# Seven block products in place of eight, in more slices of two feed-forward layers

## The chip, the cores and the metric

The kernel runs on one NeuronCore of a Trainium2 chip. The metric is the device time of one execution in microseconds (us). Engines: PE (TensorE, matmuls), PEld (its weight loads), DVE (VectorE), ACT (ScalarE), POOL (GpSimd), SP (SyncE, which here issues most DMAs).

## The reference

One inference step of a two-layer decoder, for a prompt of 1024 tokens and 8 single sample tokens that share all weights; the model width is 1024, everything is float32.

```
for l in 0, 1:
    hn  = rmsnorm(h, g[l][0])
    mix = (l == 0: gated linear recurrence   | l == 1: stick-breaking attention over a shared K/V)
          in parallel with attention over 256 memory tokens, then @ w_o[l]
    h   = h + rmsnorm(mix, g[l][1])
    h   = h + rmsnorm(swiglu(rmsnorm(h, g[l][2]), w_gu[l], w_down[l]), g[l][3])
    after layer 0: shared K/V = rmsnorm(h, g_kv) @ w_kv

swiglu(h, w_gu, w_down):
    gate, up = split(h @ w_gu)          # 1024 -> 2 x 2816
    return (silu(gate) * up) @ w_down   # 2816 -> 1024
```

Outputs are the residual streams, the recurrent states, the shared K/V and the memory K/V.

## The kernel before, in words

Activations lie transposed: 128 rows of the model dimension on the partitions, tokens along the free dimension. The tokens are cut in two halves, `g = 0` with 512 prompt tokens and `g = 1` with the other 512 and the 8 samples (520). `NG = [512, 520]`. All matmuls of projections are done in float32r with both operands split in a high and a low part (`split_w` and `split_to`: ACT makes the high part, DVE subtracts it), three matmuls for each product: high x high, high x low, low x high.

Code is written as generators, one `yield` after each step; `weave` mixes several of them in proportion to given weights, and so sets the order in which the instructions are traced. A scheduler of the language then orders the instructions of each engine by this order and by what is ready, on its own estimate of times. Queues are first in, first out.

The feed-forward of a half has 22 slices of 128 hidden units, grouped in five parts: `PARTS = [(0, 5), (5, 5), (10, 4), (14, 4), (18, 4)]` (first slice, count). Each part computes its slices (gate and up for each) and then multiplies by its rows of `w_down` for all eight blocks of 128 outputs, adding into `R`. There are three forms of a slice:

- Plain (`ffn.part` with `proj`, L218): 2 x 8 x 3 = 48 matmuls of 512 columns in the first half, or 96 of 260 in the second, in two PSUM tiles of two banks each (`mmp`). SiLU is made of Exp and Ln.
- Plain in four single banks (`gate_up_q`, L453): 96 matmuls of half the columns, SiLU from ACT's own table. Beside it `sums_w` makes the sums of activations that the third form needs, some steps after each matmul group (`side`, `steps`).
- Block (`gate_up_w`, L499): gate and up together are a 2 x 2 block matrix (512 rows of the model dimension each) times a 2 x 2 block matrix of activations (two halves of the model dimension, two halves of the tokens). Strassen's scheme in Winograd's form takes 7 block products instead of 8: 7 x 4 x 3 = 84 matmuls of half the columns. Four of the seven weights are sums of blocks of `w_gu`. They are made ahead in DRAM by `weight_sums`, eight DMAs for a part on POOL's queue, some of them accumulating; each first waits, by a one-column copy on POOL, for the tile in `now[0]`, so that the DMAs are spread over the work. The tiles `y`, `z`, `u` hold the sums of activations; `raws` and `spl` choose the buffers of the raw and the split weights.

`ffn_w` runs a feed-forward from part `first` on: `len(steps)` slices by `gate_up_q`, the rest by `gate_up_w`, and w_down in four single banks (L631; the last one of all, with other widths, L663). `set_banks(True)` closes the two-bank tiles and opens four single banks, `set_banks(False)` the other way; the new pool waits until the old one is free.

Before the change the block form is used only in the second half (`g = 1`): in layer 0 for slices 13 to 21, in layer 1 for slices 3 to 21. The other slices are plain. Around them, in order of time (second-half mixers `a1`, `b1`; first-half mixers `a0`, `b0`; `o0`, `o1` are out-projections with norms and residual):

1. `a0`: recurrence, memory attention, projection.
2. `a1.core()` beside part 0 of the first half's feed-forward in layer 0, then part 1 beside `a1.sample()` and `a1.gate()`.
3. `a1.merge()`, `a1.mem()` and `a1.mem_sample()` beside parts 2 and 3; then part 4 alone.
4. Shared K/V of the first half, `b0.heads()`; then `b0.sb()` and `b0.mem()` beside parts 0 and 1 of the second half's feed-forward in layer 0; then its parts 2 to 4 in `ffn_w`.
5. Shared K/V of the second half, `b1.heads()`; then `b1`'s attention and its samples beside parts 0 to 3 of the first half's feed-forward in layer 1.
6. `o1.mm()`, then `o1.finish()` beside part 4; then the last feed-forward in `ffn_w`, its parts 0 and 1 beside `f0.finish()` and the writing of rows.

In the samples' attention (`sample_scores`, `sample_pv`, L912 and L924) one 512 KB tile of the cache is loaded for each sample into the pool `c` (4 buffers), and DVE multiplies and reduces it. The evacuation of a w_down block into `R` is L390 (plain) or L640 (four banks).

## Time and profile before

| | |
|---|---|
| median of 3 runs | 2496.46 us (2495.56 to 2497.24) |
| the profiled execution | 2497.11 us |
| its span, first to last instruction | 2495.4 us |
| granted clock of TensorE over the span | 0.998 |
| PE, PEld busy | 2461.4, 2155.8 us |
| DVE, ACT, POOL busy | 1598.1, 1196.8, 121.9 us |
| matmuls | 15455 |
| HBM read, written | 358.76, 101.11 MB |

A matmul's record lasts from its start to a modelled end, so that records of neighbours overlap; "busy" is the time covered by at least one. The time from one matmul to the next is shorter than the mean of one and is read from long unbroken runs.

### The profile page before, as it was taken

How to read it: one execution, taken by the hardware profiler on the slowest of the kernel's cores; microseconds unless marked ns; L12 is line 12 of the kernel's file. 1: busy time of each engine (PE TensorE's matmuls, PEld its weight loads, DVE VectorE, ACT ScalarE, POOL GpSimd, SP SyncE). 2: the span in 40 equal slices, each digit the busy share in tenths (PEclk: the TensorE clock that was granted, in tenths of full speed). 3: DMA queues.
4: the chain of work that ended last, by engine and by line, in shares of the span. 5: the costliest groups of instructions: out<-in, count | busy, mean ns of one | idle time of the engine just before them, and what ended most of it. 6: DMA issues, size and time to landing. Idle time of an engine off the chain costs nothing.

```text
span 2495.4 us, 40868 instructions
## 1 busy us (share of the span) xinstructions
PE 2461.4 (99%) x15455; PEld 2155.8 (86%) x15455; DVE 1598.1 (64%) x2868; ACT 1196.8 (48%) x2289; POOL 121.9 (5%) x188
## 2 busy tenths in 40 slices
PE   8999999999999999999999999999999999999998
PEld 6888888877866898899999989977777798999998
DVE  5867556754765475665656575778677548855666
ACT  5437544243433454555544554555454345554445
POOL 1000000000010000000100100011000000000000
PEclk9999999999999999999999999999999999999999
DMA  5354666555786776566577746544343433464552
GB/s 190 111 165 119 162 184 157 132 141 150 223 204 184 197 185 194 165 156 167 134 199 193 226 140 187 160 145 144 102 140 119 122 120 114 141 186 144 148 148 73
DMA packets 521551, 391.26 MB, mean 157 GB/s; under 512 B 19973, under 2 KB 459858, under 8 KB 521354
## 3 DMA queue, kind: packets, MB, share of 16 engines
q1 hardware_dynamic: 493194, 308.94, 41.8%
q0 software_dynamic: 28160, 79.70, 13.5%
q8 instruction: 122, 2.00, 0.3%
q14 instruction: 75, 0.61, 0.1%
HBM read 358.76 MB, written 101.11 MB: 184 GB/s over the span
## 4 chain that ended last, share of the span: by engine, by line
PE 92%; DVE 4%; DMA 2%; ACT 1%; issue 1%; SPq 0%; DVEq 0%; ACTq 0%
PE mm L218 54%; PE q L499 11%; PE q L631 7%; PE s L1150 2%; PE mm L1018 2%; PE q L453 2%; PE s L1345 1%; PE s L1311 1%; PE s L885 1%; PE s L854 1%; PE mm L803 1%; PE mm L830 1%; PE q L663 1%; DMA c<-in_cache_mem_v 1%; PE ns L926 1%
## 5 line engine op out<-in xcount | busy, mean ns | idle before, releaser
L218 PE MATMUL mm<-x,ws 128*128 128x512 f32 (+1 forms) x6624 | 1215.0, 340 | 3.9 <-DVE r L390 1.5
L218 PEld LDWEIGHTS mm<-x,ws 128*128 128x128 f32 x6624 | 1012.5, 188 | 157.6 <-issue 14.6
L204 ACT CAST ws<-w 128x512 fp32r<-128x512 f32 (+1 forms) x672 | 395.3, 589 | 624.2 <-PE mm L218 477.8
L205 DVE TENSOR_TENSOR ws<-w,ws 128x512 fp32r<-128x512 f32 (+1 forms) x672 | 434.5, 650 | 270.5 <-ACT ws L204 263.8
L218 PE MATMUL mm<-m,ws 128*128 128x512 f32 (+1 forms) x1536 | 327.9, 366 | 4.7 <-DVE r L390 4.7
L218 PEld LDWEIGHTS mm<-m,ws 128*128 128x128 f32 x1536 | 253.2, 188 | 56.7 <-DVE r L390 7.3
L631 PE MATMUL q<-m,ws 128*128 128x260 f32 x1440 | 175.9, 283 | 0.0
L631 PEld LDWEIGHTS q<-m,ws 128*128 128x128 f32 x1440 | 173.4, 188 | 1.1 <-DVE t L522 0.5
L490 DVE TENSOR_TENSOR ws<-w,ws 128x512 fp32r<-128x512 f32 x164 | 112.4, 691 | 79.8 <-ACT ws L489 76.4
L489 ACT CAST ws<-w 128x512 fp32r<-128x512 f32 x164 | 101.4, 621 | 98.0 <-PE q L631 34.2
L499 PE MATMUL q<-x,ws 128*128 128x260 f32 x1008 | 134.3, 282 | 0.0
L499 PEld LDWEIGHTS q<-x,ws 128*128 128x128 f32 x1008 | 126.4, 188 | 0.0
L499 PE MATMUL q<-y,ws 128*128 128x260 f32 x912 | 119.3, 283 | 0.1
L499 PEld LDWEIGHTS q<-y,ws 128*128 128x128 f32 x912 | 113.5, 188 | 0.3 <-ACT q L506 0.3
L235 DVE TENSOR_SCALAR t<-mm 128x512 f32<-128x512 f32 (+1 forms) x70 | 48.3, 690 | 59.7 <-PE mm L218 59.4
L695 DVE TENSOR_TENSOR t<-t,mm 128x512 f32<-128x512 f32 (+1 forms) x54 | 37.2, 688 | 57.1 <-PE mm L218 57.1
L390 DVE TENSOR_TENSOR r<-r,mm 128x512 f32<-128x512 f32 (+1 forms) x72 | 49.3, 685 | 37.1 <-PE mm L218 36.2
L239 DVE TENSOR_TENSOR t<-t,t 128x512 f32<-128x512 f32 (+1 forms) x54 | 37.4, 692 | 55.1 <-ACT t L238 55.1
L226 DVE TENSOR_TENSOR m<-t,m 128x512 fp32r<-128x512 f32 (+1 forms) x88 | 60.9, 692 | 6.7 <-ACT m L225 5.3
L258 DVE TENSOR_TENSOR st<-st,n 128x512 f32<-128x512 f32 (+1 forms) x91 | 62.2, 691 | 3.0 <-ACT n L257 1.6
L225 ACT CAST m<-t 128x512 fp32r<-128x512 f32 (+1 forms) x88 | 54.9, 624 | 17.0 <-DVE t L695 7.7
L453 PE MATMUL q<-x,ws 128*128 128x260 f32 x480 | 61.0, 288 | 1.5 <-DVE ws L205 1.4
(344 smaller groups left out, 2850.5 us busy)
## 6 DMA issues: line engine op xcount, KB each, us to landing
w<-in_w_gu SPq DMA_DIRECT2D x310, 256.0 KB
w<-in_w_down SPq DMA_DIRECT2D x160, 256.0 KB
wsum<-in_w_gu POOLq DMA_DIRECT2D x36, 1024.0 KB, 9.4
w<-wsum SPq DMA_DIRECT2D x94, 256.0 KB
w<-in_w_in_a SPq DMA_DIRECT2D x80, 256.0 KB
w<-in_w_o SPq DMA_DIRECT2D x64, 256.0 KB
wsum<-in_w_gu POOLq DMA_DIRECT2D x12, 1280.0 KB, 11.4
wsum<-wsum POOLq DMA_DIRECT2D x12, 1024.0 KB, 5.6
```

What stands on the lines that cost most here:

```text
L204: nc.scalar.copy(ws[:, 0, :n, :], raw[:, :n, :])
L205: nc.vector.tensor_sub(ws[:, 1, :n, :], raw[:, :n, :], ws[:, 0, :n, :].bitcast(F32))
L218: nc.tensor.matmul(ps[:, a, : PW[g]], wt, xt[k][:, xi, o : o + PW[g]], start=(k == 0 and wi == 0), stop=(k == nk - 1 and wi == 2),)
L225: nc.scalar.copy(dst[0], src)
L226: nc.vector.tensor_sub(dst[1], src, dst[0].bitcast(F32))
L258: nc.vector.tensor_add(acc[:, :n], acc[:, :n], t[:, :n])
L453: ins = nc.tensor.matmul(pp[a][:, :h], wt, xt[k][:, xi, a * h : (a + 1) * h], start=(k == 0 and wi == 0), stop=(k == ND - 1 and wi == 2),)
L489: nc.scalar.copy(w[:, 0, :], src)
L490: nc.vector.tensor_sub(w[:, 1, :], src, w[:, 0, :].bitcast(F32))
L499: nc.tensor.matmul(ps[:, :h], w[:, wj, k * P : (k + 1) * P], x[:, xi, :], start=(first and k == 0 and wi == 0), stop=(k == 3 and wi == 2), ...
L631: nc.tensor.matmul(pp[a][:, :h], wt, mids[k][:, xi, a * h : (a + 1) * h], start=(k == 0 and wi == 0), stop=(k == nf - 1 and wi == 2),)
L1018: nc.tensor.matmul(pb[i][:, a, :], xt[k][:, xi, c * P : (c + 1) * P], ws[:, s, :], start=(k == 0 and wi == 0), stop=(k == ND - 1 and wi == 2),
```

## The change

It uses the block form for five slices of the first half in either layer (17 to 21), and for fourteen instead of nine of the second half in layer 0 (8 to 21). For that:

- `sums_w`, `gate_up_q`, `gate_up_w` and `ffn_w` take the half `g` as an argument; in the first half the columns are 256 + 256.
- Layer 0, first half: parts 3 and 4 run in an `ffn_w` of their own behind the memory attention of `a1`, with four single banks; part 2 alone stays beside that attention.
- Layer 0, second half: `ffn_w` begins with part 1 instead of part 2; part 0 alone stays beside `b0`'s attention.
- Layer 1, first half: parts 3 and 4 run in an `ffn_w` beside `o1.finish()`; parts 0 to 2 stay beside `b1`'s attention. There (`own`) the tiles `y` come from the pool `c`, and the split weights only from their own pool.
- `weight_sums` makes part 1 of layer 0 too (four parts, order 3, 4, 2, 1), and begins beside `a0.core()`, where `now[0]` is set to a tile of the recurrence. In layer 1 the order becomes 3, 4, 0, 1, 2, fewer steps stand in layer 0, and the last eight stand beside the last feed-forward's parts 0 and 1.

```diff
-    def sums_w(xs, ops, YT):
-        n, h = NG[1], PW[1]
+    def sums_w(g, xs, ops, YT, ZT):
+        n = NG[g]
+        h = n // 2
         for k in range(4):
             x0, x1 = xs[k], xs[k + 4]
             y = YT()
             if k % 2 == 0:
-                z, u = YT(), YT()
+                z, u = ZT(), ZT()
...
-    def gate_up_q(l, f, xt, side, n_side, first):
+    def gate_up_q(g, l, f, xt, side, n_side, first):
...
-    def gate_up_w(l, f, ops, spl, raws):
+    def gate_up_w(g, l, f, ops, spl, raws):
...
-        def __init__(self, l, x, steps, first, rows, R=None):
+        def __init__(self, g, l, x, steps, first, rows, R=None, own=False):
...
             def YT():
                 if rows:
                     return xpool.tile([P, 2, NG[1]], F32R, tag="x0", name=nm("y"))
+                if own:
+                    return cpool.tile([P, 2, 512], F32R, tag="c", name=nm("y"))
                 return A(F32R)
-            self.sums = sums_w(x, self.ops, YT)
+            self.sums = sums_w(g, x, self.ops, YT, YT if rows else lambda: A(F32R))
...
-            if (self.pi or not self.rows) and self.n % 8 in (1, 4, 6):
+            if (self.pi or not self.rows) and not self.own and self.n % 8 in (1, 4, 6):
                 return cpool.tile([P, 2, 512], F32R, tag="c", name=nm("ws"))
...
+                now[0] = F_[:, 0, 0:1]
                 for hh in range(2):
                     nc.vector.copy_predicated(
...
     drain(a0.v(), a0.fq())
+    w0 = weight_sums(0, (3, 4, 2, 1))
     weave(
-        (a0.core(), 22),
+        (a0.core(), 22), (islice(w0, 8), 8),
         (chain(mem_load(), mem_keys(0), mem_values(0), mem_keys(1), mem_values(1), a0.qm(M)), 22),
     )
...
-    w0 = weight_sums(0, range(2, 5))
...
-    ws = weight_sums(1, range(5))
-    weave(
-        (chain(a1.merge(), a1.mem()), 12), (a1.mem_sample(), 20), (chain(f0.part(2), f0.part(3)), 16),
-        (islice(ws, 11), 11),
-    )
-    weave((f0.part(4), 8), (islice(ws, 5), 5))
+    ws = weight_sums(1, (3, 4, 0, 1, 2))
+    weave((chain(a1.merge(), a1.mem()), 12), (a1.mem_sample(), 20), (f0.part(2), 8), (islice(ws, 4), 4))
+    set_banks(True)
+    fw = ffn_w(0, 0, o0.x, (5, 6, 5), 3, False, f0.R)
+    weave((chain(fw.part(3), fw.part(4)), 16), (islice(ws, 4), 4))
+    f0.acc = fw.acc
+    set_banks(False)
...
-    weave((chain(b0.sb(), b0.mem()), 25), (chain(f1.part(0), f1.part(1)), 18), (islice(ws, 16), 17))
+    weave((chain(b0.sb(), b0.mem()), 20), (f1.part(0), 9), (islice(ws, 16), 17))
     set_banks(True)
-    fw = ffn_w(0, o1.x, (5, 6, 5), 2, False, f1.R)
-    weave((chain(fw.part(2), fw.part(3), fw.part(4)), 24), (islice(ws, 8), 8))
+    fw = ffn_w(1, 0, o1.x, (5, 6, 5), 1, False, f1.R)
+    weave((chain(fw.part(1), fw.part(2), fw.part(3), fw.part(4)), 33), (islice(ws, 8), 8))
...
         (chain(b1.sb(), b1.mem()), 45), (chain(b1.sb_sample(), b1.mem_sample()), 39),
-        (chain(f0.part(0), f0.part(1), f0.part(2), f0.part(3)), 34),
+        (chain(f0.part(0), f0.part(1), f0.part(2)), 27),
     )
     o1 = out_proj(1, 1, A, True)
     drain(o1.mm(b1.xo))
-    weave((o1.finish(), 17), (f0.part(4), 8))
     set_banks(True)
-    f1 = ffn_w(1, o1.x, (5, 6, 5), 0, True)
-    weave((chain(f0.finish(False), store_y(0, f0.R), token_rows(1, o1.R)), 17), (chain(f1.part(0), f1.part(1)), 7))
+    fw = ffn_w(0, 1, o0.x, (5, 6, 5), 3, False, f0.R, True)
+    weave((o1.finish(), 17), (chain(fw.part(3), fw.part(4)), 16))
+    f0.acc = fw.acc
+    f1 = ffn_w(1, 1, o1.x, (5, 6, 5), 0, True)
+    weave((chain(f0.finish(False), store_y(0, f0.R), token_rows(1, o1.R)), 17), (chain(f1.part(0), f1.part(1)), 7), (ws, 4))
     drain(f1.part(2), f1.part(3), f1.part(4))
```

More of the change, by code (lines that the diff above doesn't have):

```diff
@@ L312, in rms_rows @@
         nc.vector.tensor_scalar(xt, xt, ss[:n], None, op0=ALU.mult)
-    made = [None]
+    made, now = [None], [None]
     def start(g, out):
@@ L440, in token_rows @@
         htok.append((ht, hs_))
-    def gate_up_q(l, f, xt, side, n_side, first):
-        h, n = PW[1], NG[1]
+    def gate_up_q(g, l, f, xt, side, n_side, first):
+        n = NG[g]
+        h = n // 2
         sg = T()
@@ L469, in gate_up_q @@
         return mt
-    def gate_up_w(l, f, ops, spl, raws):
-        h, n = PW[1], NG[1]
+    def gate_up_w(g, l, f, ops, spl, raws):
+        n = NG[g]
+        h = n // 2
         part, o = part_of(f)
@@ L527, in gate_up_w @@
         return mt
-    now = [None]
     act = [None]
@@ L563, in tile_decoder @@
     class ffn_w:
-        def __init__(self, l, x, steps, first, rows, R=None):
-            self.g, self.l, self.x, self.ops, self.steps, self.rows = 1, l, x, [], steps, rows
+        def __init__(self, g, l, x, steps, first, rows, R=None, own=False):
+            self.g, self.l, self.x, self.ops, self.steps, self.rows, self.own = g, l, x, [], steps, rows, own
             self.first, self.plain, self.n, self.r, self.pi = first, PARTS[first][0] + len(steps), 0, 0, 0
@@ L602, in part @@
         def part(self, pi):
-            l, n, h = self.l, NG[1], PW[1]
+            g, l, n = self.g, self.l, NG[self.g]
+            h = n // 2
             f0, nf = PARTS[pi]
@@ L609, in part @@
                 if f0 + j < self.plain:
-                    mids.append(gate_up_q(l, f0 + j, self.x, self.sums, self.steps[j], PARTS[self.first][0]))
+                    mids.append(
+                        gate_up_q(g, l, f0 + j, self.x, self.sums, self.steps[j], PARTS[self.first][0])
+                    )
                     now[0] = mids[-1][:, 0, 0:1].bitcast(F32)
                 else:
-                    mids.append(gate_up_w(l, f0 + j, self.ops, self.spl, self.raws))
+                    mids.append(gate_up_w(g, l, f0 + j, self.ops, self.spl, self.raws))
                 yield
```

## The prediction

> **What bounds the kernel now.** I read the page first: busy shares, then the engines of the chain that ended last.
>
> ```profile
> span 2495.4 us, 40868 instructions
> PE 2461.4 (99%) x15455; PEld 2155.8 (86%) x15455; DVE 1598.1 (64%) x2868; ACT 1196.8 (48%) x2289; POOL 121.9 (5%) x188
> PE 92%; DVE 4%; DMA 2%; ACT 1%; issue 1%; SPq 0%; DVEq 0%; ACTq 0%
> ```
>
> PE is idle for 2495.4 - 2461.4 = 34.0 us in all, and 92% of the chain is PE. So the time is the sum of the matmuls' spacings plus a few waits, and the change is to be priced by counting matmuls. "Busy" hides the spacing, since matmuls overlap in the records; a long unbroken run in the chain, its length divided by its count, gives it. In the chain in order of time (start, length, what, count):
>
> ```profile
> 652.85 55.64 PE mm L218 x240
> 1259.47 28.70 PE q L453 x240
> 1321.74 40.37 PE q L499 x336
> 1362.11 23.21 PE q L631 x192
> 1511.47 5.74 PE mm L218 x48
> ```
>
> The first run is the first half of the prompt, 512 columns: 55.64/240 = 231.8 ns. The others have 260 columns: gate/up of a plain slice in four banks 28.70/240 = 119.6, block products 40.37/336 = 120.1, w_down in four banks 23.21/192 = 120.9, the two-bank plain projection 5.74/48 = 119.6 ns. Two matmuls of 260 thus cost a little more than one of 512, while the block form does 7/8 of the work.
>
> What surrounds these runs, by windows (length, PE busy, PEld, DVE, ACT, POOL, clock, DMA share, GB/s):
>
> ```profile
> 690.00:828.00 138.00, 130.65 (x557) 96.46 (x556) 81.06 (x138) 50.22 (x106) 11.12 (x16) 1.00 0.73 190
> 1062.00:1250.00 188.00, 187.34 (x1446) 178.05 (x1445) 115.17 (x230) 98.03 (x203) 18.85 (x30) 1.00 0.62 153
> 1600.00:2000.00 400.00, 397.91 (x1824) 302.40 (x1822) 287.88 (x445) 193.11 (x372) 26.56 (x24) 1.00 0.43 127
> 2200.00:2430.00 230.00, 230.00 (x1917) 229.57 (x1916) 137.28 (x258) 114.39 (x233) 0.00 (x0) 1.00 0.56 161
> ```
>
> The first three are the stages from which the change takes feed-forward work that stands beside attention: call them A (memory attention of the second half and the samples, layer 0), B (stick-breaking of the first half, layer 1) and S (attention of the second half and the samples, layer 1). PE idles 7.35, 0.66 and 2.09 us in them. The last window holds block slices alone: no idle time at all, at 161 GB/s.
>
> **The change, part by part.** *First half, layers 0 and 1: slices 14 to 21 leave the plain form.* Their matmuls get 256 columns, a width that has no long run of its own. The nearest rows are the two widths of the last w_down, by form:
>
> ```profile
> L663 PE MATMUL q<-m,ws 128*128 128x264 f32 x96 | 12.1, 286 | 0.0
> L663 PE MATMUL q<-m,ws 128*128 128x256 f32 x96 | 11.9, 283 | 0.1
> ```
>
> Eight columns less are worth 0.2 us/96 = 2.1 ns of busy time or 3 ns of one's mean; four less, 1 to 1.5 ns. The slope between 512 and 260, (231.8 - 120.1)/252 = 0.44 ns a column, gives 1.8. I take 1.5: 118.1 plain, 118.6 block, 119.4 w_down. The far end is no saving from the narrower width. Per layer:
> - Slices 17 to 21, five: 48 x 231.8 = 11.13 us becomes 84 x 118.6 = 9.96, -1.17 each, -5.8.
> - Slices 14 to 16, three, plain in four banks so that the operand sums can be made beside them: 96 x 118.1 = 11.34, +0.21 each, +0.6.
> - w_down of parts 3 and 4: 96 x 231.8 = 22.25 becomes 192 x 119.4 = 22.92, +0.67 each, +1.3.
>
> That is -3.9 a layer, -7.7 for both; with no saving from the width (2 x 1092 x 1.5 ns) it is -4.4.
>
> *Second half, layer 0.* Block slices 8 to 21 instead of 13 to 21: five go from 96 matmuls at 119.6 (11.48) to 84 at 120.1 (10.09), -1.39 each, -7.0. Part 1's w_down keeps its count.
>
> Matmuls together: -14.7.
>
> *Operand sums*: `sums_w` now runs four times instead of two. One run, by groups of 1225 to 1265 us, and that window:
>
> ```profile
> L296 DVE TENSOR_TENSOR b<-b,b 128x260 f32<-128x260 f32 x16 | 6.7, 420 | 0.0
> L226 DVE TENSOR_TENSOR a<-b,a 128x260 fp32r<-128x260 f32 x16 | 6.6, 421 | 0.5 <-ACT a L225 0.5
> L288 DVE TENSOR_TENSOR b<-x 128x260 f32<-128x260 f32 x16 | 6.3, 420 | 0.0
> 1225.00:1265.00 40.00, 40.00 (x331) 39.57 (x330) 33.14 (x81) 19.44 (x44) 5.19 (x5) 1.00 0.95 226
> ```
>
> 19.6 us of DVE each, and PE lost nothing under it; without that cover it would be 19.6 each. One of the new runs stands alone (layer 0): 0. The other stands beside `o1.finish()`, whose DVE work competes; its nearest likeness is the same step in the last feed-forward:
>
> ```profile
> 2130.00:2187.00 57.00, 56.19 (x454) 55.61 (x455) 43.13 (x90) 29.71 (x68) 0.00 (x0) 0.97 0.51 151
> ```
>
> 0.81 us of idle PE: +0.8.
>
> *Weights.* A block slice splits seven tiles instead of four, ACT and DVE, and loads 7 x 256 KB on SP's queue instead of 4; 15 slices make 45 more of each. By groups of 1300 to 1420 us:
>
> ```profile
> L490 DVE TENSOR_TENSOR ws<-w,ws 128x512 fp32r<-128x512 f32 x28 | 19.3, 691 | 15.5 <-ACT ws L489 14.2 <-DMA w<-wsum 1.1
> L489 ACT CAST ws<-w 128x512 fp32r<-128x512 f32 x28 | 17.3, 619 | 22.8 <-DMA w<-wsum 7.9 <-PE q L631 6.9 <-PE q L499 5.0
> ```
>
> One product takes PE 12 x 118.6 = 1.42 us, the split 0.62 and 0.69 on two engines, and the 2200 window ran so without a gap: 0. If that cover failed, a late split would hold PE for its 1.31 us, 45 of them for 59. Layer 0 gets eight more weight-sum steps on POOL's queue (four parts for three), the first eight now beside `a0.core()`, paced by a mark on its tile `F_`.
>
> ```profile
> wsum<-in_w_gu POOLq DMA_DIRECT2D x36, 1024.0 KB, 9.4
> 62.00:187.00 125.00, 124.32 (x813) 110.45 (x812) 89.16 (x208) 51.40 (x92) 0.00 (x0) 1.00 0.46 139
> 640.00:710.00 70.00, 70.00 (x306) 56.65 (x305) 48.79 (x69) 28.40 (x47) 6.79 (x10) 1.00 0.83 234
> ```
>
> At 0.46 the DMA engines have room there (at 0.83, in the third row, PE still lost nothing): 0. In layer 1 the last eight steps (part 2) move behind everything else on POOL's queue, past the page gathers, to the last stage; slice 10 of the last feed-forward then waits for them, and SP's queue with the next loads behind it. Eight steps at 9.4 us are 75; the two parts that stand before that slice are ten slices (11.5 and 10.1 us) and two w_down of 29, some 165 us: 0, with about 90 to spare if the steps keep pace with the slices they follow.
>
> *Bank switches*: two more changes to four banks and two back. The way in shows no gap inside the 1225 window. The way back, on PE's timeline:
>
> ```profile
> 1449.73 2.56 PE L218 MATMUL mm<-x,ws 128*128 128x512 f32 x10 [0.90 <-DVE r L640]
> ```
>
> 0.9 each, +1.8. Block slices use Silu where the plain form uses Exp and Ln, and `o1.finish()` needs Ln and Exp between them, so ScalarE changes tables more often:
>
> ```profile
> L464 ACT ACT_TABLE_LOAD  x2: 1283/1283/1283, 1261.1 to 2120.1; - x2
> ```
>
> Up to four extra loads, 5.1 us of an engine that is half idle: 0 on the path. The Trainium skill, "ScalarE: Activation LUTs", section "What ACT_TABLE_LOAD costs", has the same 1283 ns and adds a drain of about 1380; by it the four would be 10.6 us of ScalarE (an estimate from that page), which no row here can show.
>
> *Cover.* Stage A keeps one part of two, B one of two, S three of four; the parts' PE time is only moved, but attention's waits have less beside them. In A, waits of 640 to 828 us and their pieces of the chain:
>
> ```profile
> DVE c L924 <- DMA c<-in_cache_mem_v: 14.7, 6, 4.5
> DVE c L912 <- DMA b<-qd: 8.0, 2, 7.6
> PE mm L218 <- DVE r L390: 6.2, 3, 3.0
> ```
>
> DVE, in order, stands waiting for a sample's load, behind it the evacuation `r` (L390) of a w_down block, and PE waits for that bank. The number of loads stays; the work between two of them halves. If PE's reserve hides as much as now the loss stays at 7.35; if nothing is hidden, all 22.7 us of DVE's waits reach PE, +15.4. Below nothing: if the block part fills these gaps, up to -7.35. I take half as much again, +3.7. B and S have a surplus at their ends, runs of parts with no attention left between:
>
> ```profile
> 1228.79 24.95 PE mm L218 x209
> 1949.03 11.31 PE mm L218 x48
> 1986.97 5.75 PE mm L218 x24
> ```
>
> In S these are the first and the last of five such runs, from 1949 to 1993 us, so 44 of the part's 4 x 11.13 + 22.25 = 66.8 us covered nothing. By the same half: +0.3 and +1.0 (ends -2.8 and +8).
>
> Sum: -14.7 + 0.8 + 1.8 + 3.7 + 1.3 = -7.1. The profiled execution took 2497.1 (its span and 1.7 around it), 0.65 above the median of the runs; 2497.1 - 7.1 = 2490.0, which I leave at 2490 for the median too.
>
> **Rivals.** *The gain arrives whole*: parts lifted out run clean, like the 2200 window, and the gaps of A shrink instead of growing. For it: 0 idle wherever four banks are used; against: A's waits are on transfers. -14.7 + 2.6 - 2 or so: 2483.
>
> *Cover lost eats it*: A at +8, B and S at +5 with the 2.6 of switches and sums: +15.6, so 2498. For it: DVE already waits 22.7 us in A; against: the surpluses.
>
> *Slower*: DVE becomes the bound of A. Its groups and the window of 640 to 828 us:
>
> ```profile
> L205 DVE TENSOR_TENSOR ws<-w,ws 128x512 fp32r<-128x512 f32 x55 | 37.6, 686 | 8.6 <-ACT ws L204 8.6
> L390 DVE TENSOR_TENSOR r<-r,mm 128x512 f32<-128x512 f32 x20 | 13.7, 684 | 9.8 <-PE mm L218 9.6
> L239 DVE TENSOR_TENSOR t<-t,t 128x512 f32<-128x512 f32 x8 | 5.5, 689 | 5.9 <-ACT t L238 5.9
> 640.00:828.00 188.00, 180.65 (x775) 136.99 (x774) 119.33 (x190) 71.74 (x142) 15.70 (x22) 1.00 0.75 207
> ```
>
> It has 119.3 us of work there now, and part 3's share is 24 splits (L205), 8 evacuations (L390) and 16 others at about 0.69, 33 us. What is left, 86, plus 22.7 of waits that come twice as densely and double, is 131, and 19.6 of operand sums if the block part is pulled in beside them: 151, against 188 - 67 = 121 of PE. All 30 reach PE: -14.7 + 2.6 + 1.3 + 30 = +19, 2516. It decides from the point where A loses 11 us more than now, and shows as slower from 16. Against it: PE held full at 48.79 of 70 DVE in the 640 window.
>
> *Weight loads are the bound at this width*, a mechanism that would leave 256 columns at the price of 260: PEld is busy 229.57 of 230 us in the block window, and only 56.65 of 70 at 512 columns. The 3.3 us of width are then missing: 2493.3. For it that row, against it the 1 to 1.5 ns of the L663 pair. The Trainium skill, "TensorE: Matmul & The Clock Gate", section "LDWEIGHTS (loading the stationary operand)", gives columns/1.2, 107 ns for 128, about what 256 columns take; by it narrower matmuls stop paying just here, and the 120 ns of the trace lie above that floor.
>
> **How the numbers follow.** No change means within 0.2%, 5.0 us, of 2496.5; about the least that can be told apart here. The forecast as worked out (2486 to 2494) 0.38; gain whole (under 2486) 0.22; weight loads with it 0.10; cover lost (2494 to 2502) 0.16; DVE bound in A (above) 0.14. Of the first, 0.30 lies below 2491.5, and of the weight loads' case 0.04: faster 0.30 + 0.22 + 0.04 = 0.56; same 0.08 + 0.06 + 0.16 = 0.30; slower 0.14. The range 2480 to 2502 leaves out the slower case and a sliver below; the likeliest case alone is 2486 to 2494.
>
> **What would show it.** Right: L218 at 512 columns falls by 1152, L499 grows by 1260 (15 x 84), runs of L499 at 256 columns near 118.6 ns; idle PE in A about 11 us; no PE wait on wsum. Wrong: runs at 256 columns above 120 ns; PE waits on `r` or on `c` in A above 18 us; DVE near full there; idle PE in S above 10 us; a wait of the last feed-forward at slice 10.

## The result, and the profile after

The changed kernel takes 2518.79 us (median of 4, 2515.82 to 2520.81) against 2496.01 (median of 4, 2494.68 to 2497.24) for the kernel before on the same chip: 1.009 of it, 95% interval 1.0074 to 1.0106. It is slower by 22.8 us where 2490 was forecast, and above the range. The profiled execution took 2515.82; executions of one kernel differ by up to some 0.4%, and where a profile below is of one far from its median, its time stands beside the reading.

The head of the page after:

```profile
span 2513.7 us, 43236 instructions
PE 2458.4 (98%) x16427; PEld 2198.7 (87%) x16427; DVE 1644.4 (65%) x3059; ACT 1226.4 (49%) x2396; POOL 146.4 (6%) x204
```

Idle time of PE rises from 34.0 to 55.3 us, and busy PE falls by only 3.0. To see what lies under "busy", I summed over all matmuls the median distance from one start to the next of their kind (line and shape): some 2420 us before and 2404 after. So the matmuls did become about 16 us cheaper (15 to 18 by how the kinds are drawn), and, with a span that is 18.3 us longer, what is lost between and inside them rose by some 34.

Where, by windows whose ends are the same matmuls in both kernels: A from its first transpose of the memory samples to the first transpose of the out-projection's norm, B from `b0.sb()` to the end of layer 0's second half, S from `b1.sb()` to the first transposed residual row of the store. Columns: window, its length, busy PE, PEld, DVE, ACT, POOL, clock, DMA share, GB/s. Before:

```profile
652.80:943.50 290.70, 283.26 (x1373) 226.34 (x1372) 190.81 (x298) 124.88 (x231) 22.92 (x32) 1.00 0.74 201
1035.20:1455.80 420.60, 419.05 (x3335) 406.73 (x3334) 250.18 (x477) 206.66 (x408) 37.90 (x56) 1.00 0.67 175
1597.00:2196.60 599.60, 594.97 (x3149) 482.43 (x3148) 419.50 (x683) 297.95 (x572) 26.56 (x24) 1.00 0.42 127
```

After, with the window of the first core (62 to 187 us) ahead of them:

```profile
62.00:187.00 125.00, 120.11 (x776) 106.92 (x775) 87.41 (x203) 49.45 (x88) 8.22 (x14) 0.99 0.69 194
659.90:945.10 285.20, 281.09 (x1889) 250.13 (x1888) 211.29 (x380) 134.99 (x271) 14.70 (x16) 0.99 0.61 175
1036.80:1465.80 429.00, 416.15 (x3274) 402.58 (x3273) 255.84 (x505) 212.73 (x433) 43.97 (x56) 0.99 0.72 191
1607.10:2214.50 607.40, 593.99 (x3666) 503.68 (x3665) 439.25 (x765) 311.31 (x614) 39.24 (x32) 1.00 0.47 138
```

A is shorter by 5.5 us, as hoped for or better. B is longer by 8.4 where it should be 6.7 shorter, S longer by 7.8. A starts 7.1 later (659.9 for 652.8), and that is lost in the first core: PE's idle time there is 4.89 us, 0.68 before. What follows S takes the same time in both. 7.1 - 5.5 + 8.4 + 7.8 = 17.8 of the 18.3 us of span.

How such a loss looks, in B, on the timeline after (start, length, engine, line, what, idle time before it and its releaser; lines in between left out):

```profile
1299.28 1.04 POOL L556 DMA_DIRECT2D wsum<-in_w_gu  x1
1299.72 9.27 PE L638 MATMUL q<-m,ws 128*128 128x260 f32 x76
1303.33 0.37 SPq L487 DMA_DIRECT2D w<-wsum  x1
1312.07 0.62 ACT L492 CAST ws<-w 128x512 fp32r<-128x512 f32 x1 [8.12 <-DMA w<-wsum]
1312.72 0.69 DVE L493 TENSOR_TENSOR ws<-w,ws 128x512 fp32r<-128x512 f32 x1 [7.54 <-ACT ws L492]
1313.33 0.75 DVE L647 TENSOR_TENSOR r<-r,q 128x260 f32<-128x260 f32 x2
1313.80 2.44 PE L638 MATMUL q<-m,ws 128*128 128x260 f32 x9 [4.80 <-DVE r L647]
```

Read from the bottom: PE waits 4.80 us for a bank of w_down that DVE has not evacuated (L647). Its matmuls ran until 1309.0, so the evacuation had what it needed by then; but ahead of it in DVE's order stands the split of the next slice's tile (L493), which waits for ACT's half of the split, which waits for a load. That load was issued at 1303.3 and, by the chain, landed 8.71 us later, at 1312.05. Ahead of all this POOL issued a weight-sum step. The DMA queues from 1302 to 1308 us, and from 1309 to 1315 (packets, MB, share of the 16 engines' time), q1 being SP's and q0 POOL's:

```profile
q0 software_dynamic: 419, 1.07, 96.0%
q1 hardware_dynamic: 204, 0.10, 8.7%
```

```profile
q1 hardware_dynamic: 2484, 1.23, 77.1%
q0 software_dynamic: 12, 0.01, 0.5%
```

While the step is in flight SP's queue moves 0.10 MB in 6 us; once it is through, 1.23. A packet of q0, as the trace counts them, has 1.07 MB/419 = 2.6 KB and its record lasts 0.96 x 16 x 6 us/419 = 220 ns; one of q1 has 0.5 KB and, by the same division, 41 ns. The Trainium skill, "DMA: Bandwidth & Descriptors", section "Queues, rings and completion order", says that each engine takes turns between the queues it has work for, a whole packet at a time; its packet holds some 9 to 17 descriptors, and that this is what the trace counts as one is not shown. Were the turns one record for one, and had q1 work for every engine all the time, q1 would keep 41/261 of an engine, 16% (an estimate worked out from these two durations and that page). The trace agrees in kind, and is harsher: 8.7% of the engines' time, one record for two.

And the price goes on behind the pause:

```profile
1309.00:1313.80 4.80, 0.00 (x1) 0.00 (x1) 1.08 (x3) 1.66 (x3) 0.00 (x0) 0.99 0.92 243
1313.80:1317.20 3.40, 3.40 (x15) 3.35 (x16) 2.15 (x5) 0.00 (x0) 0.00 (x0) 0.52 0.52 153
```

These are the pause and the stretch after it. For 3.4 us the granted clock is 0.52, and 15 matmuls run where 28 of 120 ns would: another 1.6 us. The records show such stretches for 10 us of the kernel before and for 27 of the changed one (the end of the span left out). The Trainium skill, "TensorE: Matmul & The Clock Gate", section "What's actually happening", has the clock halved after an idle window of about 3.4 us that runs freely, and given back after a busy one of the same length; the 3.4 us of half rate behind the 4.80 us of pause agree with it.

The theory from here on: *the weight-sum DMAs, 1 or 1.25 MB each, hold up SP's loads wherever they run, and the change put eight of them beside the first core and others beside stages that are close behind their loads*. The main rival is the forecast's own: *cover is lost where the feed-forward no longer stands beside attention*, cover being PE work that fills attention's waits. All comparisons below are with runs of the kernel before on the same chip, whose median lay between 2493.66 and 2496.01.

### The profile page after: what moved, and what is told of

Same layout as the page of the kernel before. It is cut to its first block, busy times and chain, and to the rows that moved or that the text cites. A ratio compares the mean times of both kernels' runs of the same rounds, so it can differ in the third digit from the quotient of the medians.

```text
span 2513.7 us, 43236 instructions
## 1 busy us (share of the span) xinstructions
PE 2458.4 (98%) x16427; PEld 2198.7 (87%) x16427; DVE 1644.4 (65%) x3059; ACT 1226.4 (49%) x2396; POOL 146.4 (6%) x204
## 4 chain that ended last, share of the span: by engine, by line
PE 45%; DVE 4%; DMA 3%; ACT 1%; issue 1%; SPq 0%; POOL 0%; DVEq 0%; ACTq 0%
PE q L502 14%; PE mm L218 14%; PE q L638 9%; PE q L455 2%; PE q L670 1%; DMA w<-wsum 1%; PE s L1319 1%; DMA w<-in_w_down 1%; PE s L1353 1%; DMA b<-qd 1%; PE ns L933 1%; PE s L892 0%; DVE ws L205 0%; DVE b L1339 0%; PE s L861 0%
## 5 line engine op out<-in xcount | busy, mean ns | idle before, releaser
L218 PE MATMUL mm<-x,ws 128*128 128x260 f32 (+1 forms) x5376 | 973.9, 337 | 3.6 <-DVE t L235 1.9
L218 PEld LDWEIGHTS mm<-x,ws 128*128 128x128 f32 x5376 | 809.7, 188 | 119.5 <-issue 13.8
L204 ACT CAST ws<-w 128x512 fp32r<-128x512 f32 x612 | 357.6, 586 | 523.2 <-PE mm L218 322.4
L205 DVE TENSOR_TENSOR ws<-w,ws 128x512 fp32r<-128x512 f32 x612 | 392.4, 646 | 271.8 <-ACT ws L204 260.0
L638 PE MATMUL q<-m,ws 128*128 128x260 f32 (+1 forms) x2448 | 301.7, 284 | 7.9 <-DVE r L647 7.9
L638 PEld LDWEIGHTS q<-m,ws 128*128 128x128 f32 x2448 | 297.2, 190 | 10.6 <-DVE r L647 8.6
L493 DVE TENSOR_TENSOR ws<-w,ws 128x512 fp32r<-128x512 f32 x216 | 148.4, 690 | 111.6 <-ACT ws L492 108.2
L218 PE MATMUL mm<-m,ws 128*128 128x512 f32 (+1 forms) x912 | 210.5, 377 | 0.0
L502 PE MATMUL q<-x,ws 128*128 128x260 f32 (+1 forms) x1548 | 206.2, 282 | 0.4 <-ACT t L515 0.4
L492 ACT CAST ws<-w 128x512 fp32r<-128x512 f32 x216 | 133.6, 621 | 134.0 <-PE q L638 42.6
L502 PEld LDWEIGHTS q<-x,ws 128*128 128x128 f32 x1548 | 193.6, 188 | 1.1 <-ACT t L515 0.6
L218 PEld LDWEIGHTS mm<-m,ws 128*128 128x128 f32 x912 | 153.6, 189 | 35.1 <-issue 7.9
L502 PE MATMUL q<-a,ws 128*128 128x260 f32 (+1 forms) x1032 | 134.6, 282 | 2.5 <-DVE t L468 2.2
L502 PE MATMUL q<-y,ws 128*128 128x260 f32 (+1 forms) x1032 | 135.4, 283 | 0.1
L502 PEld LDWEIGHTS q<-a,ws 128*128 128x128 f32 x1032 | 128.0, 188 | 3.0 <-DVE t L468 2.4
L455 PEld LDWEIGHTS q<-x,ws 128*128 128x128 f32 x960 | 115.2, 188 | 0.2
L647 DVE TENSOR_TENSOR r<-r,q 128x260 f32<-128x260 f32 (+1 forms) x176 | 66.5, 419 | 61.5 <-PE q L638 61.2
L493 DVE TENSOR_TENSOR ws<-b,ws 128x512 fp32r<-128x512 f32 x85 | 58.4, 690 | 29.7 <-ACT ws L492 28.1
```

Of the source, the lines that this page charges most:

```text
L204: nc.scalar.copy(ws[:, 0, :n, :], raw[:, :n, :])
L205: nc.vector.tensor_sub(ws[:, 1, :n, :], raw[:, :n, :], ws[:, 0, :n, :].bitcast(F32))
L218: nc.tensor.matmul(ps[:, a, : PW[g]], wt, xt[k][:, xi, o : o + PW[g]], start=(k == 0 and wi == 0), stop=(k == nk - 1 and wi == 2),)
L455: ins = nc.tensor.matmul(pp[a][:, :h], wt, xt[k][:, xi, a * h : (a + 1) * h], start=(k == 0 and wi == 0), stop=(k == ND - 1 and wi == 2),)
L492: nc.scalar.copy(w[:, 0, :], src)
L493: nc.vector.tensor_sub(w[:, 1, :], src, w[:, 0, :].bitcast(F32))
```

## The experiments

**e1: the eight steps beside the first core moved to the recurrence's sample stage.**

```
-        (a0.core(), 22), (islice(w0, 8), 8),
+        (a0.core(), 22),          # its 8 steps run with the later (w0, 5)
```

> The changed kernel with the first eight weight-sum steps of layer 0 taken from beside a0.core(); they follow with the last ones, beside a1.sample(), a1.gate() and part 1. Theory Q (while an accumulating weight-sum DMA is in flight on POOL's queue, SP's loads and stores hardly move, so each such step is a hole of 6 to 9 us in SP's traffic): the loss of PE beside the core (7.2 us over the sum of the median spacings in the changed kernel, 1.2 before) goes back to about 1, together -5 to -6 us against the changed kernel (2518.8), some 2513, if the new place is free. Theory C (cover: what the change lost is attention with too little work beside it): nothing changes beside the core, 2518 to 2520.

2540.74 us (4 runs), 1.0176 [1.0159, 1.0193]: far above both forecasts. The first core is free again (0.1 us behind the kernel before at 491 us), but the steps moved run into the memory samples, and PE pauses there, above all so (waits of 660 to 760 us, in an execution that took 2546.81):

```profile
PE mm L218 <- DVE ws L205: 9.2, 1, 9.2
```

**e2: no steps beside B's block slices.** The sums of part 1 are left out and part 0's taken in their place.

```
-    ws = weight_sums(1, (3, 4, 0, 1, 2))
+    ws = weight_sums(1, (3, 4, 0, 2))        # and sums[1][1] = sums[1][0]
-    weave((chain(fw.part(1), ... fw.part(4)), 33), (islice(ws, 8), 8))
+    weave((chain(fw.part(1), ... fw.part(4)), 33))
```

> The changed kernel without the eight weight-sum steps that stand beside the second half's block slices in layer 0 (1.25 MB each, sums of part 1 of layer 1); the last feed-forward then takes part 0's sums for part 1 as well, so that its loads are as many. Left out: these eight DMAs and their results. Theory Q: the block slices of that stage lose about 3 us of PE instead of 16.9, the three pauses of 2.5 to 5 us go: 2503 to 2508. Theory W (a rival: the block slices' own traffic, 7 tiles a slice, is too much for SP's queue and for the splits, the sums only happen to be there): 2516 to 2519.

2502.77 us (9 runs), 1.0032 [1.0022, 1.0042], just under the 2503 to 2508 of the theory: 16 us come back from eight DMAs (14 to 15 by the two ratios). B in its profile:

```profile
1038.70:1453.90 415.20, 412.36 (x3276) 399.51 (x3274) 256.70 (x505) 213.15 (x433) 25.60 (x40) 1.00 0.64 172
```

415.2 us instead of 429.0, though the 16 steps ahead, beside `b0.sb()`, are still there: those cost nothing (with no step at all B takes 415.3, e13 below), the eight beside the block slices 13.8.

**e3: layer 1 of the first half as before.**

```
-        (chain(f0.part(0), f0.part(1), f0.part(2)), 27),
+        (chain(f0.part(0), f0.part(1), f0.part(2), f0.part(3)), 34),
...
-    weave((o1.finish(), 17), (chain(fw.part(3), fw.part(4)), 16))
+    weave((o1.finish(), 17), (f0.part(4), 8))
```

> The changed kernel with the first half of layer 1 as before: all of parts 0 to 3 plain beside b1's attention, part 4 beside o1.finish(). Theory C for this stage: PE's loss beside b1's attention falls from 17.2 to 9 us and beside o1.finish() by 3, the matmuls cost 3.9 more: about -7, some 2512. Theory Q alone (the sums are the whole loss): no sum runs in that stage, so only the matmuls come back: +4, some 2523.

2516.75 us (4 runs), 1.0084 [1.0067, 1.0101]: between the two forecasts, and not told from the changed kernel. In its profile (an execution of 2522.88, 6 us above the median) S falls only 1.6 us behind the kernel before up to the place that it has at 2092 us, but then the eight steps of the last place meet the store of the residual, and 7.5 us go there. What was gained in one place was lost in another, and the total decides nothing between the two theories.

**e4: the kernel before with eight unused steps beside the first core**, and **e11: the same, all eight plain copies.**

```
+    we = weight_sums(0, (1,))
-        (a0.core(), 22),
+        (a0.core(), 22), (we, 8),
```

> The kernel before with eight weight-sum steps of 1.25 MB (part 1 of layer 0) added beside a0.core(), paced as in the changed kernel; nobody uses them. It is the disputed cost by itself. Theory Q: PE loses about 6 us there, 2501 to 2503 against 2496. Rival (the loss beside the core came from another order of the instructions, or there is room for these DMAs, as predicted): 2495 to 2498.

> The kernel before with 8 unused DMAs of 1.25 MB beside the recurrence's first core, as in e4 (2504.1), but all 8 plain copies and none that accumulates. Theory 'an accumulating DMA is what holds the load queue up': 2496 to 2499, and no pause over 1.5 us between 83 and 190 us in the profile. Rival 'any DMA of 1.25 MB from that queue does, whatever it does with the data': 2501 to 2506, with a pause of some 5 us as e4 had at 106 us.

e4 took 2504.13 us (6 runs), 1.0036 [1.0024, 1.0049], some 9 us more than before and 1 more than the theory's 2501 to 2503: the steps alone make the loss of the first core, with no feed-forward changed. In the chain and in PE's waits of 95 to 120 us:

```profile
101.79 8.92 DMA mks<-t
```

```profile
PE mm L811 <- ACT t L808: 5.2, 1, 5.2
```

Here the transfer that stands still is a store of the memory keys, whose buffer ACT needs. With plain copies, e11, it is 2502.47 (7 runs), 1.0029 [1.0017, 1.004]: the same within the intervals. That half of them add into their target, which I held to be the cause, is not needed: plain copies of that size from that queue do it too. The pause itself is less clear in e11: its profile is of an execution of 2497.11, and PE waits there for 2.1 us where e4 has 5.2.

**e5: each weight-sum DMA cut into four of 128 rows, each with its own mark**, the same bytes and the same matmuls; **e10: into eight of 64 rows; e9: the kernel before, cut into four.**

```
-                mark = nc.gpsimd.tensor_copy(small([P, 1], ...), now[0])
-                with tc.issue_after(mark.ins):
-                    nc.gpsimd.dma_start(d, a, ...)
-                yield
+                for r in range(0, 512, 128):
+                    mark = nc.gpsimd.tensor_copy(small([P, 1], ...), now[0])
+                    with tc.issue_after(mark.ins):
+                        nc.gpsimd.dma_start(d[r : r + 128], a[r : r + 128], ...)
+                    yield
```

> The changed kernel with every weight-sum step cut into four of 128 rows (256 or 320 KB), each with its own mark, so that the same bytes go in holes a quarter as long. Theory Q in its form that the length of one hole against PE's reserve decides: the losses beside the core (7.2) and in the second half's block slices of layer 0 (16.9) fall to 2 and 4, together about -18: 2499 to 2503. Rival (the bytes decide, or the accumulation itself): 2515 to 2521.

> The changed kernel with its weight-sum DMAs cut into eight of 64 rows (e5 has four of 128 rows). Theory 'the load queue stands for as long as one such DMA lasts': with 128 rows the hold is some 2 us and under the loads' lead, so a further cut gains nothing: 2488 to 2493. Rival 'the fixed cost of more marks and DMAs on GpSimd begins to count': 2495 to 2505. Third way, 'the rest of the lost time still comes from these DMAs': 2480 to 2486.

> The kernel before the change, with each of its own weight-sum DMAs (64 of 1 MB or 1.25 MB) cut into four of 128 rows, each with its own mark; same bytes, same matmuls. It says what the change is worth once its DMAs are cut. Theory 'the long weight-sum DMAs hold the load queue up, and the change only added more of them': the kernel before loses little to them in its profile (half clock 10 us of its span, pauses of 7.9 us in its 652 to 944 us), so it gains at most some 10 us: 2484 to 2494; and since 16 us of matmuls separate it from the change with cut DMAs at 2490.75, that one is faster only if this stays above 2491. Rival 'the change's worth of 15 us comes through once the DMAs are cut': this one then lies 10 to 15 us above 2490.75, at 2496 or more, with nothing gained by the cut. In the profile: pauses over 1.2 us between 550 and 944 us gone by the theory, as before by the rival.

e5: 2490.75 us (10 runs), 0.9983 [0.9973, 0.9992]. Twenty-eight microseconds of the changed kernel's time (27 by the two ratios) go away, 8 more than the best that was expected, with the matmuls and the bytes as they were. e10 gains nothing that can be told from it: 2489.01 (10 runs), 0.9981 [0.9972, 0.999]. q0 of e5 moves the same 90 MB, and one of its pieces of 256 KB lands 5.9 us after its issue, where a whole DMA of 1 MB took 9.4:

```profile
q0 software_dynamic: 34816, 90.20, 16.3%
wsum<-in_w_gu POOLq DMA_DIRECT2D x144, 256.0 KB, 5.9
```

A piece holds up SP's queue as a whole step does, but for less long. In e5's block slices POOL issued one at 1282.23 us, the next 5.4 us later and the one ahead of it 10 us earlier; the queues from 1284 to 1286 us, and from 1286 to 1288:

```profile
q0 software_dynamic: 84, 0.21, 86.8%
q1 hardware_dynamic: 28, 0.01, 2.2%
```

```profile
q1 hardware_dynamic: 903, 0.45, 76.1%
q0 software_dynamic: 57, 0.11, 32.2%
```

So the cut changed two things at once: each hold is some 2 us instead of 6 to 9, and the holds stand apart. No run separates the two.

But e9 also gains: 2491.59 (11 runs), 0.9987 [0.9978, 0.9996]. (Its profile, of 2493.34, still has one pause of 2.7 us in A for an evacuation, 3.0 the longest before; by the theory it should have gone.) With whole DMAs the change costs 22.8 us; with cut ones it is worth 0.8, which is no difference. So cutting did not bring back the forecast's gain, and something else still eats most of the 16 us of matmuls.

**e6: another order of layer 1's sums**, so that the steps beside B's block slices move 1 MB instead of 1.25.

```
-    ws = weight_sums(1, (3, 4, 0, 1, 2))
+    ws = weight_sums(1, (3, 0, 1, 4, 2))
```

> The changed kernel with the parts of layer 1's sums in the order 3, 0, 1, 4, 2, so that the eight steps beside the second half's block slices are of 1 MB (part 4) instead of 1.25 MB (part 1). Theory Q, hole against reserve: three holes of about 6.5 instead of 8.5 us, the pauses of 2.5, 5 and 3 us shrink by about 2 each and the half-clock stretches behind them go: -6 to -10, 2509 to 2513. If the place alone decides, whatever the size: 2517 to 2520.

2515.03 us (4 runs), 1.0077 [1.006, 1.0093]: between the two, and its interval holds the changed kernel. A fifth fewer bytes a step settles nothing.

**e7: B's eight steps moved on, beside `b1.heads()`; e12 and e15: the last place's steps moved back, in small ones**, with layer 1 of the first half as before (that base is **e8**, both edits of e3 and e5 together).

```
e7   -    weave((chain(fw.part(1), ...), 33), (islice(ws, 8), 8))
     +    weave((chain(fw.part(1), ...), 33))
     -    weave((b1.heads(), 8), (o0.finish(), 17))
     +    weave((b1.heads(), 8), (o0.finish(), 17), (islice(ws, 8), 8))
e12  -    weave((chain(fw.part(1), ...), 33), (islice(ws, 32), 32))
     +    weave((chain(fw.part(1), ...), 33), (ws, 64))
e15  -        (chain(f0.part(0), f0.part(1), f0.part(2), f0.part(3)), 34),
     +        (chain(f0.part(0), f0.part(1), f0.part(2), f0.part(3)), 34), (ws, 32),
```

> The changed kernel with those eight steps (1.25 MB) moved behind the second half's block slices, beside b1.heads() and o0.finish(), where weights of plain slices are loaded. Theory Q with a free place: as without them, 2503 to 2507. If such a step costs wherever it is put (each hole 1 to 2 us): 2510 to 2518.

> The small steps together with the first half of layer 1 as before. If both effects add: about 6 us less than with the small steps alone, 2493 to 2497, about the kernel before or a little under it. If the loss beside b1's attention was itself due to late sums: no less than with the small steps alone.

> The changed kernel with its weight-sum DMAs cut into four, layer 1 of the first half as in the kernel before (this is e8, 2489.8), and the last eight steps (32 small ones) moved from beside the last residual stores to beside the block slices of layer 0's second half, which then carry 64 small ones in 280 us. Theory 'a step costs where it meets loads that are close behind their use, and the last place is such a one': e8 lost 4.9 us there (from -13.8 against the kernel before at 2155 us to -8.9 at 2197), and with half as many bytes a microsecond again beside the block slices nothing is lost there: 2484 to 2486. Rival 'what is moved costs the same again where it goes', as e7 showed for whole steps: 2488 to 2493. In the profile: the load of in_w_down that ScalarE waited 8.2 us for at 2158 us is gone by the theory; by the rival a pause or half clock stands between 1160 and 1440 us.

> The changed kernel with its weight-sum DMAs cut into four and layer 1 of the first half as in the kernel before (e8, 2489.8), and the last 32 small steps moved from beside the residual stores to beside the 480 us of the sparse attention that stands ahead of them, where the DMA engines are 0.39 to 0.48 busy (0.70 to 0.73 beside the block slices, where e12 put them). Theory 'small steps cost nothing where the DMA engines have half their time free': the 4.9 us of the last place come back, 2484 to 2486. Rival 'they cost the same wherever they are put', now through the page gathers that share their queue: 2488 to 2493, with a wait for in_cache_sb_k or in_cache_sb_v of over 3 us between 1590 and 2080 us.

e7: 2518.82 us (4 runs), 1.0089 [1.0072, 1.0106], no gain. In its profile (an execution of 2525.85) B's end is back (0.7 us behind the kernel before, 10.0 in the changed one), and at the start of S PE stands for 10.6 us, for a load of the keys:

```profile
PE s L1319 <- DMA a<-ksc: 10.6, 1, 10.6
```

e8: 2489.78 us (6 runs), 0.9972 [0.996, 0.9985], against 2490.75 with layer 1 in its new form, where 6 us less would have shown that the two effects add. So that part of the change is worth nothing even with short DMAs. e8 loses 4.9 us in the last place; in its chain of 2130 to 2210 us:

```profile
2157.99 8.21 DMA w<-in_w_down
```

e12: 2489.87 (11 runs), 0.9984 [0.9975, 0.9993], and e15: 2490.96 (11 runs), 0.9989 [0.998, 0.9998]; 2484 to 2486 was expected of both by the theory, and the rival holds. In e12 S, last place included, is back to 599.8 us, but B takes 423.3, and in e15 B stays at 418.3 and S takes 607.8. The windows of B and S, of e12 and then of e15, and of e15 the wait of DVE in S that is new:

```profile
1022.70:1446.00 423.30, 413.96 (x3275) 399.84 (x3274) 255.75 (x505) 212.02 (x433) 140.75 (x264) 1.00 0.83 213
1587.30:2187.10 599.80, 593.73 (x3149) 480.93 (x3148) 419.10 (x683) 297.91 (x572) 26.25 (x24) 1.00 0.42 126
```

```profile
1020.90:1439.20 418.30, 413.78 (x3274) 399.88 (x3273) 256.36 (x505) 212.88 (x433) 108.77 (x200) 1.00 0.75 196
1580.50:2188.30 607.80, 596.29 (x3150) 481.88 (x3149) 418.21 (x683) 297.33 (x572) 60.59 (x88) 1.00 0.48 138
```

```profile
DVE c L932 <- DMA c<-in_cache_sb_v,pidx: 10.6, 3, 5.9
```

The DMA engines are 0.48 busy in S and 0.83 in B; the steps cost 8.0 us in the one (607.8 for 599.8) and 4.3 in the other (423.3 for 419.0 in e8). The mean share of a stage does not say what a step costs there. In S the new wait is for the page gathers, which stand behind the steps on POOL's queue (10.6 us with a longest of 5.9, against 5.7 with a longest of 1.9 in e12).

**e13 and e14: both kernels without any weight-sum DMA**, the blocks loading columns of the weights in the sums' place.

```
-            sums.setdefault(l, {})[i] = (s1, s2, s3, s4)
+            sums.setdefault(l, {})[i] = (a21, a22, a11, a12)
-            for d, a, add in (...):         # mark and DMA
+            for _ in range(8):
                 yield
```

> The changed kernel with all its weight-sum DMAs and their marks left out; the blocks load columns of the weights themselves in the sums' place (same number, size and order of loads and matmuls; the sums, and so the block products, are left out). Read as a pair with the kernel before treated in the same way (e14). If the added weight-sum DMAs are all that ate the 16 us of matmuls, the pair lies 14 to 17 us apart. If cover also went in layer 1 of the first half, as the 16.0 us lost there even with cut DMAs say (9.3 before), the pair lies 7 to 12 us apart: this one 2476 to 2484. If the gain is not to be had even without those DMAs, the pair lies within 3 us.

> The kernel before with all its weight-sum DMAs and their marks left out, and columns of the weights loaded in the sums' place (the sums, and so the block products, are left out). Its partner is e13. Cutting the DMAs into four gained 2.8 us (e9), so that they are all but hidden here: 2485 to 2492 by that. Rival, that even before the change they held up more than cutting could give back: under 2484.

The two are read as a pair. e13: 2478.26 us (5 runs, 2475.85 to 2481.44), 0.9935 [0.9922, 0.9949]. e14: 2484.55 (5 runs, 2481.97 to 2485.68), 0.9952 [0.9939, 0.9966]. Without these DMAs the change is a gain: every run of e13 is below every run of e14, by 6.3 us between the medians and 4.2 by the two ratios. That is less than the 7 to 12 expected if cover went too, and more than the 3 expected if there were nothing to gain. e14 itself lies just under the 2485 to 2492 of its forecast. The table of medians; its rows come from different sets of runs, in which the kernel before had medians from 2493.66 to 2496.01, so that a difference between rows is good to some 2 us:

| weight sums | before | changed | difference |
|---|---|---|---|
| whole DMAs | 2496.01 | 2518.79 | +22.8 |
| cut in four | 2491.59 | 2490.75 | -0.8 |
| none | 2484.55 | 2478.26 | -6.3 |

Down the columns: those DMAs cost 40.5 us in the changed kernel (39 by the ratios) and 11 to 12 in the one before; cut in four, 12.5 and 7.0. By stage, A, B and S of e13 and then of e14:

```profile
647.90:927.50 279.60, 278.75 (x1892) 248.88 (x1891) 211.56 (x379) 135.88 (x272) 0.00 (x0) 1.00 0.50 148
1019.20:1434.50 415.30, 412.42 (x3275) 399.58 (x3274) 256.43 (x505) 213.22 (x433) 8.11 (x8) 1.00 0.43 126
1575.70:2177.60 601.90, 593.39 (x3665) 503.16 (x3664) 439.83 (x765) 311.13 (x614) 29.23 (x24) 1.00 0.44 133
```

```profile
649.90:932.50 282.60, 282.43 (x1376) 227.18 (x1375) 192.16 (x298) 125.58 (x232) 0.00 (x0) 1.00 0.44 133
1024.90:1445.30 420.40, 418.69 (x3334) 406.52 (x3333) 250.48 (x477) 207.09 (x408) 8.10 (x8) 1.00 0.39 115
1586.50:2185.50 599.00, 593.64 (x3149) 480.85 (x3148) 419.28 (x683) 297.99 (x572) 26.82 (x24) 1.00 0.42 126
```

A gains 3.0 us, B 5.1, and S loses 2.9 although its matmuls are 4 to 5 cheaper by their median distances: some 7 us are lost there that no weight-sum DMA can have cost. PE's waits in S, 1576 to 2100 us, in e13 and in e14:

```profile
PE s L1338 <- ACT b L1332: 3.7, 5, 2.5
PE s L875 <- DVE b L868: 2.1, 2, 1.1
```

```profile
PE s L1330 <- ACT b L1324: 1.7, 5, 0.4
PE s L868 <- DVE b L861: 0.4, 1, 0.4
```

The same five waits of score matmuls (`ACT b`) are longer, one of them 2.5 us, and 3.4 us of half clock stand behind it. So both theories hold, each in its place: the DMAs in the first core, in B and in the last place, as runs show that add or remove them there; and in S lost cover, which is read from these waits, since no run without weight sums puts layer 1 alone back.

No version is better than the cut ones: e8, e10, e5, e12 and e15 lie at 0.9972 to 0.9989 of the kernel before with overlapping intervals, and so does e9, which has nothing of the change.

## Why the prediction was wrong

*Matmuls: -14.7.* Right. The counts came as forecast: L218 at 512 columns went from 4224 to 3072, the block form from 2352 to 3612. The width did too. On PE's timeline of the changed kernel, a plain slice in four banks, the first group of the block that follows its last one, the w_down behind the blocks, and one w_down of stage A, all at 256 columns:

```profile
2003.08 28.61 PE L455 MATMUL q<-x,ws 128*128 128x256 f32 x240
2031.53 1.59 PE L502 MATMUL q<-x,ws 128*128 128x256 f32 x12
2041.54 18.63 PE L638 MATMUL q<-m,ws 128*128 128x256 f32 x154
867.65 23.04 PE L638 MATMUL q<-m,ws 128*128 128x256 f32 x192
```

From start to start, (2031.53 - 2003.08)/240 = 118.5 ns plain, (2041.54 - 2031.53)/84 = 119.2 block, and 23.04/192 = 120.0 w_down, where 118.1, 118.6 and 119.4 stood: 0.4 to 0.6 ns short of the saving that was taken. They are 0.9 to 1.1 ns below the 260 columns, so the width did not stay at the price of 260, as the rival of the weight loads had it. All matmuls together: about -16.

*Weight-sum DMAs beside the first core: 0.* This is the step that failed, together with the next term. "At 0.46 the DMA engines have room there" took the mean share of a window for the room between a load and its use. The stage loses 6 to 7 us (7.1 in the changed kernel's profile, half clock included), because a single step all but stops SP's queue for 6 to 9 us, whatever the mean. The page of the profile had the sign of it: 9.4 us to land for 1 MB, and nothing in the sum asked what SP's queue does in those 9.4.

*Weights of the block slices: 0.* "The 2200 window ran so without a gap" was true of a window with no weight-sum step in it (POOL 0.00 there). In B the eight steps run beside the same slices: 13.8 us by e2. All 64 steps of the kernel before cost only 11 to 12 us by e14, so that its profile gave little warning; still, ACT's half of the split was quoted with 7.9 us of waits for wsum, and that was the row to follow. The prediction also named the price of a failed cover, 59 us for 45 splits; what failed was not every split a little but a few by 5 us, with the evacuation behind them.

*The last eight steps: 0, with 90 us to spare.* Slice 10 did not wait. But the steps collided with the store of the residual and the loads of w_down: 4.9 us in e8, and not much cheaper in either other place (4.3 in e12, 8.0 in e15). The term asked whether the sums come in time, not what they push aside.

*Cover in A: +3.7.* Wrong in the safe direction: PE's idle time in A fell from 7.44 to 4.11 us, and its waits for an evacuation `r` from 6.2 to 0.8. All that PE waits for in A after:

```profile
PE ns L933 <- DVE c L932: 3.3, 1, 3.3
PE mm L218 <- DVE r L647: 0.8, 1, 0.8
```

Without any weight sums A gains 3.0, against +0.7 by the terms (-3.9 for matmuls, +3.7 cover, +0.9 for the bank switch). *In B +0.3*: 5.1 gained for 6.7, near. *In S +1.0*, its far end being +8 for B and S: some 7 were lost. The "surplus" of 44 us without attention was at the stage's end, while the waits are spread over it; what stands beside each wait is what counts, as far as the waits of e13 and e14 show it.

*Bank switches, +1.8*: a miscount. The kernel before already changes to four banks twice and back once, and the change adds one of each, not two: layer 0's second half had both, and in layer 1 the switch only moves ahead. PE's wait at the way back (`r` at L218) is 1.7 us in two places after and 0.9 in one before, so +0.8. *Operand sums, +0.8*: not measured apart.

So the terms for the change itself came to -7.1, and the pair without weight-sum DMAs measures -6.3 (-4.2 by the ratios). That they lie so close is luck in part: A came out 3.7 us better than its terms, S some 5 worse, B 1.6 worse. The term of 0 for the DMAs was off by some 27 to 29 us. Of the rivals, the slower one (2516) came closest in time, by a mechanism that did not happen: DVE is no bound in A. None of the rivals put the new waits on the queue of loads.

Left open: why 64 whole DMAs cost the kernel before only 11 to 12 us and 72 cost the changed one 40. The steps beside `b0.sb()` cost nothing and those beside block slices 1.7 us each, so place decides, but the runs give no rule that tells the places apart ahead of time; the mean DMA share is not one. Open as well: whether the cut helps by shorter holds or by holds that stand apart, and why q1 gets fewer turns than q0.

## What to carry to other kernels

Price a background DMA by what its one transfer does to the queue it competes with, not by the mean share of the DMA engines: here a transfer of 1 to 1.25 MB all but stopped the other queue for 6 to 9 us, and the same bytes in pieces of 128 rows, each with its own mark, gave 28 us back. An in-order engine that evacuates PSUM must not stand behind a split that waits for a load. And before a gain in matmuls is credited, list the stages in which the moved work had covered waits, and look at what lies beside each wait, not at the stage's totals.

## What the hardware showed that I had not expected

- Two DMA queues on the same 16 engines are far from fair: 1.07 MB against 0.10 in 6 us, packets of 2.6 KB and 220 ns against 0.5 KB and 41 ns. The loss of time does not need an adding DMA (e11).
- A pause of PE of 4 us or more has a price behind it as well, 1.6 us in B. In the changed kernel each of the three (4.2, 4.8 and 5.1 us) is followed by 3.4 us at a granted clock of 0.50 to 0.52; behind a wait of 2.9 us it stays at 1.00 in one place (1725 us) and is 0.50 in another (1379 us). The changed kernel had 27 us of such stretches; e5 in its profile, an execution of 2485.6, had none but at its end. Part of the spread between executions goes with it: of e5's ten, those of 2485.6 and 2486.72 us have a granted clock of 1.0, those of 2490.18 to 2493.31 have 0.997 or 0.998, and the one of 2494.33, at 0.999, does not fit.
